# The first block's second mixer written as a pipeline in a kept order, one head a step, with scores from stacked fp32r parts

## The chip, the core and the metric

The kernel runs on one core of one Trainium2 chip. The metric is the device time of one execution in microseconds. PE is the matmul engine, DVE the vector engine, ACT the scalar engine, POOL the GpSimd engine and SP the engine that issues most DMAs.

## What is computed

The whole program is two blocks of two layers on 256 positions of width 1024. The change is in the mixer of the first block's second layer: an input projection, 16 heads with three attention branches each (compressed, selected, window), and an output projection. At 256 positions all four blocks of 64 are selected and the window covers everything, so the selected and the window branch are both causal attention, over keys of their own (`ks`, `kw`).

```python
def nsa_mixer(h, w_in, b_gate, q_g, k_g, cmp_pos, cmp_w1, cmp_w2, rel_table, w_out):
    q, kc, vc, ks, vs, kw, vw, gl = jnp.split(h @ w_in, splits, axis=-1)
    q = rms_norm(q.reshape(B, S, G, J, Dh), q_g)
    ks = rms_norm(ks, k_g[1])
    kw = rms_norm(kw, k_g[2])
    gates = jax.nn.sigmoid((gl + b_gate).astype(f32)).reshape(B, S, G, J, 3)
    Kc = rms_norm(compress(kc, cmp_pos[0], cmp_w1[0], cmp_w2[0]), k_g[0])
    Vc = compress(vc, cmp_pos[1], cmp_w1[1], cmp_w2[1])
    s_c = jnp.einsum('bsgjd,bngd->bgjsn', q, Kc) * scale + table[...]
    p_c = masked_softmax(s_c, ends[None, :] <= tpos[:, None])
    o_c = jnp.einsum('bgjsn,bngd->bsgjd', p_c, Vc)
    ...
    s = jnp.einsum('bqgjd,bqgnld->bgjqnl', qi, Kg) * scale + bias      # selected blocks
    o_s = jnp.einsum('bgjqnl,bgqnld->bqgjd', masked_softmax(s, m), Vg)
    ...
    s = jnp.einsum('bqgjd,bkgd->bgjqk', qi, kb) * scale + bias_w       # window
    o_w = jnp.einsum('bgjqk,bkgd->bqgjd', masked_softmax(s, mask), vb)
    ...
    o = gates[..., 0:1] * o_c + gates[..., 1:2] * o_s + gates[..., 2:3] * o_w
    return o.reshape(B, S, NSA_WIDTH) @ w_out
```

## The kernel before

`odd_mixer` computes this mixer. Weights come in **units** of 128x1024: `E.units` loads two units in one DMA, and `E.split` (L171) makes of each an fp32r high part `w_hi` (a copy on ACT, L175) and a low part `w_lo` (a subtraction on DVE or POOL, L166; `E.pattern` says which). A unit is 24 matmuls of 128x256 in fp32r: `mm3` (L201) issues three products for each of eight blocks.

The stage that the change touches begins when the keys, the values and the gates have been computed. Eight query units fill `q` (four in each call of `queries`); after each, `head_stat` adds the sum of squares with a small matmul, and after four the factors of the normalization are worked out by `rstd` and `rows` (L254 to L259, L369, L370), spread over the partitions by `spread2` (L386) and multiplied in. `attend(a)` then runs eight heads. It first computes the compressed branch of all eight (L1282 to L1305), and then for each head: two score matmuls in plain fp32 with a contraction of 64 (L1314, L1316), four DVE operations that add the bias and find the maximum (L1327), four exponentials on ACT with their sums (L1329), the scaling by gate and sum (L1331 to L1336), six transposes (L1339 to L1341) with two copies out (`pts`, L1344 on ACT and L1346 on DVE), and five matmuls with the values into `pv` (L1348 to L1351). After every second head `E.parts` reads `pv` into `yh` (ACT, L488) and `yl` (DVE, L489). Eight output units then accumulate into `acc` from `yh` and `yl`.

The order is the scheduler's: it may move instructions across heads and units. The pools limit it: the scores have two PSUM buffers (`at`), the transposes one (`tp`), `pv` one, the weights three of `w_hi` and three of `w_lo`.

## Time and profile before

| | us |
|---|---|
| median of 3 runs | 3491.49 (3486.87 to 3491.85) |
| the profiled execution | 3472.96 |
| its span, first to last instruction | 3471.2 |
| PE busy | 3306.5 (95%) |
| DVE busy | 2408.9 (69%) |
| ACT busy | 1895.5 (55%) |
| POOL busy | 944.4 (27%) |

The span holds all stages. The stage of this change lies at about 1114 to 1265 us, one twenty-third of it. PE counts as busy from the start of a matmul to its modelled end, so a stage with PE near 100% can still hold slow matmuls; what a matmul costs is better read from the distance between the starts of two neighbours.

### The profile page before, as it was taken

To read this page: it belongs to the slowest core of one execution; us is meant where nothing else is said; L and a number is where in the kernel's file an instruction comes from. 1 tells how busy PE (TensorE), PEld (TensorE's weight loads), DVE (VectorE), ACT (ScalarE), POOL (GpSimd) and SP (SyncE) were. 2 spreads that over 40 slices of the span, in tenths; PEclk is the share of its full clock that TensorE was granted. 3 is DMA by queue.
4 is the path that set the end of the run, shared out by engine and by line. 5 is a ranking of instruction groups with operands and counts; after the bars stand their busy time and mean duration, and the time that the engine had idled before them with its cause. 6 is when DMAs were issued, how large, how long until landed. Compare 5 with 4: busy or idle time off the path is not lost.

```text
span 3471.2 us, 64306 instructions
## 1 busy us (share of the span) xinstructions
PE 3306.5 (95%) x25971; PEld 3122.5 (90%) x25971; DVE 2408.9 (69%) x4479; ACT 1895.5 (55%) x3609; POOL 944.4 (27%) x470
## 2 busy tenths in 40 slices
PE   5889999999998999999999999999989999999899
PEld 4679999999997679999999999987869999878799
DVE  5777878888885567878867776576655454776644
ACT  3445677644445555677644445456654454565543
POOL 1034000044444135000044444442142232312422
PEclk8989999999999999999999999999999999999999
DMA  6535444477774124444345555543325555423354
GB/s 244 182 126 183 170 146 146 146 260 273 274 261 167 43 81 171 174 147 149 144 178 186 190 184 194 185 159 113 122 88 193 183 182 182 152 98 134 108 184 146
DMA packets 85979, 576.90 MB, mean 166 GB/s; under 512 B 9919, under 2 KB 11312, under 8 KB 20144
## 3 DMA queue, kind: packets, MB, share of 16 engines
q1 hardware_dynamic: 82448, 567.35, 45.7%
q8 instruction: 203, 3.33, 0.4%
q0 software_dynamic: 1648, 3.56, 0.4%
q10 hardware_dynamic: 1584, 1.88, 0.2%
q14 instruction: 96, 0.79, 0.1%
HBM read 571.80 MB, written 1.34 MB: 165 GB/s over the span
## 4 chain that ended last, share of the span: by engine, by line
PE 82%; DVE 9%; ACT 4%; issue 1%; DMA 1%; POOL 1%; ACTq 0%; DVEq 0%; POOLq 0%
PE acc L204 14%; PE acc L203 14%; PE acc L205 14%; PE mm L204 9%; PE mm L203 9%; PE mm L205 9%; PE g L1003 2%; ACT w_hi L175 2%; PE g L1005 2%; DVE w_lo L166 1%; DMA w_raw<-peer_v 1%; DVE m L1543 1%; DVE wl L489 1%; DVE xl L290 1%; DVE sql L489 1%
## 5 line engine op out<-in xcount | busy, mean ns | idle before, releaser
L175 ACT ACTIVATE w_hi<-w_raw 128x1024 fp32r<-128x1024 f32 x980 | 1037.6, 1059 | 968.9 <-PE acc L204 404.1
L166 POOL TENSOR_TENSOR w_lo<-w_raw,w_hi 128x1024 fp32r<-128x1024 f32 x357 | 865.0, 2424 | 2301.1 <-ACT w_hi L175 1507.7
L166 DVE TENSOR_TENSOR w_lo<-w_raw,w_hi 128x1024 fp32r<-128x1024 f32 x623 | 766.9, 1231 | 316.2 <-ACT w_hi L175 298.9
L203 PE MATMUL mm<-xh,w_hi 128*128 128x256 f32 (+1 forms) x2568 | 730.8, 285 | 15.2 <-ACT xh L336 7.1
L204 PE MATMUL mm<-xl,w_hi 128*128 128x256 f32 (+1 forms) x2568 | 731.8, 285 | 3.6 <-DVE xl L290 1.6
L205 PE MATMUL mm<-xh,w_lo 128*128 128x256 f32 (+1 forms) x2568 | 729.0, 284 | 2.2 <-DVE w_lo L166 2.2
L204 PE MATMUL acc<-wl,w_hi 128*128 128x256 f32 x2048 | 574.8, 281 | 8.1 <-DVE wl L489 8.0
L203 PE MATMUL acc<-wh,w_hi 128*128 128x256 f32 x2048 | 574.1, 280 | 3.3 <-ACT wh L488 3.3
L205 PE MATMUL acc<-wh,w_lo 128*128 128x256 f32 x2048 | 573.8, 280 | 0.0
L203 PEld LDWEIGHTS mm<-xh,w_hi 128*128 128x128 f32 (+1 forms) x2568 | 489.3, 191 | 23.3 <-issue 11.6
L204 PEld LDWEIGHTS mm<-xl,w_hi 128*128 128x128 f32 (+1 forms) x2568 | 489.0, 190 | 10.3 <-DVE xl L290 5.3
L205 PEld LDWEIGHTS mm<-xh,w_lo 128*128 128x128 f32 (+1 forms) x2568 | 489.3, 191 | 5.0 <-DVE w_lo L166 3.4
L203 PE MATMUL acc<-xh,w_hi 128*128 128x256 f32 (+1 forms) x1536 | 445.4, 290 | 11.6 <-DVE x L447 6.3
L204 PE MATMUL acc<-xl,w_hi 128*128 128x256 f32 (+1 forms) x1536 | 441.1, 287 | 15.5 <-DVE xl L558 15.0
L489 DVE TENSOR_TENSOR wl<-ring,wh 128x256 fp32r<-128x256 f32 x256 | 360.0, 1410 | 122.8 <-ACT wh L488 122.6
L205 PE MATMUL acc<-xh,w_lo 128*128 128x256 f32 (+1 forms) x1536 | 438.2, 285 | 0.1
L204 PEld LDWEIGHTS acc<-wl,w_hi 128*128 128x128 f32 x2048 | 385.9, 188 | 9.9 <-DVE wl L489 9.9
L203 PEld LDWEIGHTS acc<-wh,w_hi 128*128 128x128 f32 x2048 | 385.9, 188 | 3.7 <-ACT wh L488 3.7
L205 PEld LDWEIGHTS acc<-wh,w_lo 128*128 128x128 f32 x2048 | 385.9, 188 | 0.0
L204 PEld LDWEIGHTS acc<-xl,w_hi 128*128 128x128 f32 x1536 | 296.4, 193 | 19.0 <-DVE xl L558 16.9
L203 PEld LDWEIGHTS acc<-xh,w_hi 128*128 128x128 f32 x1536 | 298.1, 194 | 14.1 <-ACT xh L556 6.3
L205 PEld LDWEIGHTS acc<-xh,w_lo 128*128 128x128 f32 x1536 | 295.5, 192 | 1.3 <-DVE w_lo L166 0.4
(464 smaller groups left out, 5923.4 us busy)
## 6 DMA issues: line engine op xcount, KB each, us to landing
w_raw<-ffn SPq DMA_DIRECT2D x132, 1024.0 KB, 4.8
w_raw<-peer_u SPq DMA_DIRECT2D x128, 1024.0 KB, 4.8
w_raw<-peer_v SPq DMA_DIRECT2D x128, 1024.0 KB, 4.8
w_raw<-mix_in SPq DMA_DIRECT2D x48, 1024.0 KB, 4.8
ring<-ada SPq DMA_DIRECT2D x56, 512.0 KB, 5.8
ada<-ada SPq DMA_DIRECT2D x20, 1024.0 KB, 4.8
w_raw<-mix_out SPq DMA_DIRECT2D x16, 1024.0 KB, 4.8
w_raw<-even_in SPq DMA_DIRECT2D x12, 1024.0 KB, 6.8
```

The source lines that it names most:

```text
L166: ins = e.tensor_tensor(out, a, hi, op=OP.subtract)
L175: self.nc.scalar.activation(hi[:, :n], src, AF.Copy)
L203: mm(ps, wh, xh, start=start, stop=False, skip_group_check=True)
L204: mm(ps, wh, xl, start=False, stop=False, skip_group_check=True)
L205: mm(ps, wl, xh, start=False, stop=stop, skip_group_check=True)
L290: nc.vector.scalar_tensor_tensor(self.xl[:, c], self.x[:, c], a(c), self.xh[:, c].bitcast(F32), op0=OP.mult, op1=OP.subtract)
L489: return self.nc.vector.tensor_tensor(yl, src, yh.bitcast(F32), op=OP.subtract).ins
L1003: nc.tensor.matmul(ps[:, t], oi[:, :, t], o1[:, :, t], start=t == 0, stop=False, skip_group_check=True)
L1005: nc.tensor.matmul(ps[:, t], oi[:, :, t], o2[:, :, t], start=False, stop=t == TB - 1, skip_group_check=True)
L1543: nc.vector.scalar_tensor_tensor(m[:, sl], m[:, sl], col[:, 3 + k, h:h + 1], cbm[:, g, sl], op0=OP.mult, op1=OP.mult)
```

## The change

The stage becomes a pipeline whose order is kept as written on PE, DVE and ACT (`E.in_order`, which was there before and is used elsewhere). Three things are new.

**Scores from stacked parts.** `keys` splits the keys of a group into fp32r high and low parts, each on both halves of the partitions (`ksh`, `ksl`); `stack` puts the high part of a head's queries on one half of the partitions and the low part on the other (`qs`). `scores` then has four fp32r matmuls with a contraction of 128 (two of 256 columns, two of 512) in the place of two fp32 matmuls with a contraction of 64.

**One head a step.** Step `i` scales head `i-1`, multiplies head `i-2` with the values, turns head `i-1` (transposes), weighs head `i` (bias, maximum, exponentials), and computes the scores of head `i+1`. In steps 0 to 3 and from 8 on, half a unit of weights (12 matmuls) stands between the two turns: the last two query units, then the output units; the last three output units stand alone at the end. `scale`, `weigh`, `turn` and `values` are the old operations in functions of their own; `factors` and `scaled` are the normalization's two halves, `stats` its small matmuls.

**Where weights are split.** `Flow` splits a unit when one is finished (`flow.split`), with all subtractions on DVE. `units` at the end of an odd step is such a place.

```diff
+        qs = S.tile([128, 16, T], F32R, name="qs")
...
-            C = ctx3.enter_context(tc.tile_pool(name="cmp", bufs=1, reuse_waits="tile"))
+            C = ctxc.enter_context(tc.tile_pool(name="cmp", bufs=1, reuse_waits="tile"))
...
+        P = ctx.enter_context(tc.tile_pool(name="odp", bufs=1, reuse_waits="tile"))
+        ks = [P.tile([128, 4, 512], F32R, name=n) for n in ("ksh", "ksl")]
+        ctx.enter_context(E.in_order(*(e.engine for e in (nc.tensor, nc.vector, nc.scalar))))
+        flow = Flow(E, chain(units, E.units(io["odd_out"])), 2)
+        squares, heads, pcts, pvs = deque(), {}, {}, {}
+        def keys(g):
+            a, o = g // 2, g % 2 * 64
+            key, hi = kcat[o:o + 64, a], ks[0][o:o + 64, g]
+            for to in (o, 64 - o):
+                nc.scalar.activation(ks[0][to:to + 64, g], key, AF.Copy)
+            for to in (o, 64 - o):
+                nc.vector.tensor_tensor(ks[1][to:to + 64, g], key, hi.bitcast(F32), op=OP.subtract)
+        def keep(u, ps):
+            nc.scalar.activation(turned(q[:, u]), tiles(ps), AF.Copy)
+            sq = E.nrm.tile([128, T], F32, name="sq", bufs=4)
+            nc.scalar.activation(sq, q[:, u], AF.Square)
+            squares.append((u % 4, sq))
...
+        def stack(u):
+            for hf in range(2):
+                o = 64 * hf
+                nc.scalar.activation(qs[o:o + 64, 2 * u + hf], q[o:o + 64, u], AF.Copy)
+            for hf in range(2):
+                o = 64 * hf
+                nc.vector.tensor_tensor(qs[64 - o:128 - o, 2 * u + hf], q[o:o + 64, u],
+                                        qs[o:o + 64, 2 * u + hf].bitcast(F32), op=OP.subtract)
...
-                    mm_(s0[:, :256], q[o:o + 64, u, 0:128], kcat[o:o + 64, a, 0:256], start=True, stop=True)
-                    mm_(s1, q[o:o + 64, u, 128:256], kcat[o:o + 64, a], start=True, stop=True)
...
+        def scores(i):
+            a, j, hf, u, h = place(i)
+            qh = qs[:, 2 * u + hf]
+            s0, s1 = (at.tile([128, 512], F32, name="at") for _ in range(2))
+            for ps, ts, n in ((s0[:, :256], slice(0, 128), 256), (s1, slice(128, 256), 512)):
+                for k in range(2):
+                    mm_(ps, qh[:, ts], ks[k][:, 2 * a + hf, :n], start=k == 0, stop=k == 1)
...
+        def unit():
+            n, w = counter[0], next(flow)
+            counter[0] += 1
+            if n < 8:
...
+                    E.mm3(ps, w[0][:, c * 128:c * 128 + 128], ..., c == 0, c == NB - 1)
+                    if c == 3:
+                        yield
+                flow.split()
+                keep(n, ps)
+            else:
...
+                    E.mm3(acc[n // 2][:, n % 2], w[0][:, sl], w[1][:, sl], yh[:, k], yl[:, k], ...)
+                    if n == 3:
+                        yield
+                flow.split()
+            yield
...
-        queries(0)
-        attend(0)
-        queries(1)
...
-        attend(1)
-        E.pattern = "P"
-        units = E.units(io["odd_out"])
-        for k in range(8):
-            E.accum(acc, next(units), yh[:, k], yl[:, k], k == 0, k == 7)
+        for u in range(4):
+            for _ in unit():
+                pass
+            stats(stat, 1)
+            keys(u)
+        fill = unit()
+        next(fill)
+        stats(stat)
+        r = factors(stat, rows[0])
+        next(fill)
+        fill = unit()
+        next(fill)
+        for us in ((0, 1), (2, 3)):
+            scaled(0, r, us)
+        next(fill)
+        stack(0)
...
+        comp = compressed(0)
+        next(comp)
+        scores(0)
+        next(comp)
+        next(comp, None)
+        for i in range(18):
+            if i == 8:
+                ctx3.close()
+                acc = E.accs(...)
+            if 0 <= i - 1 < 16:
+                scale(i - 1)
+            if 0 <= i - 2 < 16:
+                values(i - 2)
+            if 0 <= i - 1 < 16:
+                turn(i - 1, 0)
+            done = i >= 3 and i % 2 == 1
+            if done:
+                u = (i - 2) // 2
+                nc.scalar.activation(yh[:, u], pvs[u], AF.Copy)
+            if i < 16:
+                weigh(i)
+            filled = i < 4 or i >= 8
+            if filled:
+                if i % 2 == 0 or i >= 16:
+                    fill = unit()
+                next(fill)
+            if 0 <= i - 1 < 16:
+                turn(i - 1, 1)
+            if done:
+                nc.vector.tensor_tensor(yl[:, u], pvs[u], yh[:, u].bitcast(F32), op=OP.subtract)
+            if i % 2 == 0 and i < 14:
+                stack(i // 2 + 1)
+            if i >= 16:
+                next(fill)
+            if i < 15:
+                scores(i + 1)
+            if i == 2:
+                stats(stat)
+            elif i == 4:
+                stats(stat)
+                r = factors(stat, rows[1])
+            elif i == 5:
+                for us in ((0, 1), (2, 3)):
+                    scaled(1, r, us)
+                comp = compressed(1)
+                next(comp)
...
+        while counter[0] < 16:
+            for _ in unit():
+                pass
```

The words below: `p_...` are a head's weights before and after scaling, `at` its scores, `pv` the output of two heads, `y_...` the parts `yh` and `yl`, `nm` and `sm` maxima and sums.

On DVE, around the reading of `pv` after every second head, before and then now:

```order
L1327 ISA p_13896,nm<-at,bias 128x2x128
L1327 ISA nm 128x1
L489 TENSOR_TENSOR y_12433<-pv,y_12433 128x256 [waits Activation_49]
L1331 RECIPROCAL sm<-sm 128x4 [waits Activation_49]
L1332 TENSOR_TENSOR sm<-sm,gates 128x4 [waits DVE_49]
L1336 TENSOR_SCALAR p_13895<-p_13895,sm 128x128 [waits DVE_49]
```

```order
L1375 ISA p_14080,nm<-at,bias 128x2x128
L1375 ISA nm 128x1
L166 TENSOR_TENSOR w_lo<-w_raw,w_hi 128x1024 [waits DMAHW5_49,Activation_49]
L1490 TENSOR_TENSOR y_12433<-pv,y_12433 128x256 [waits PE_49]
L1383 RECIPROCAL sm<-sm 128x4
L1384 TENSOR_TENSOR sm<-sm,gates 128x4 [waits DVE_49]
L1388 TENSOR_SCALAR p_14079<-p_14079,sm 128x128 [waits DVE_49]
```

A subtraction for weights, which waits for ACT, now stands ahead of the one that reads `pv` last.

On ACT, before and then now, around a copy `w_hi` in the second half of the heads (the exponentials of one head are four rows):

```order
L1329 ACTIVATE p_14016,sm<-p_14016,nm 128x2x128 [waits DVE_49]
L175 ACTIVATE w_hi<-w_raw 128x1024 [waits DMAHW6_49,PE_49,Pool_49]
L488 ACTIVATE y_12433<-pv 128x256 [waits PE_49]
L1344 ACTIVATE pts<-tp 128x3x128 [waits PE_49,Activation_49]
L1344 ACTIVATE pts<-tp 128x3x128 [waits DVE_49,PE_49,Activation_49]
```

```order
L1399 ACTIVATE pts<-tp 128x3x128 [waits PE_49,Activation_49]
L1479 ACTIVATE y_12433<-pv 128x256
L1377 ACTIVATE p_14079,sm<-p_14079,nm 128x128 [waits DVE_49]
L1377 ACTIVATE p_14080,sm<-p_14080,nm 128x2x128 [waits DVE_49]
L1377 ACTIVATE p_14079,sm<-p_14079,nm 128x128 [waits DVE_49]
L1377 ACTIVATE p_14080,sm<-p_14080,nm 128x2x128 [waits DVE_49]
L175 ACTIVATE w_hi<-w_raw 128x1024 [waits DMAHW5_49]
L1399 ACTIVATE pts<-tp 128x3x128 [waits PE_49,Activation_49] x2
```

The copy `w_hi` now stands behind the four exponentials of the step and ahead of the copies `pts` of the next turns.

On PE, in the second half of the heads, before (matmuls of a unit stand between the pieces of a head, some in the middle of three products) and then now:

```order
L1314 MATMUL at<-kcat,q 128x256 [waits DVE_49]
L1316 MATMUL at<-kcat,q 128x512 [waits DVE_49]
L1348 MATMUL pv<-pts,vr 64x256 [waits DVE_49,Activation_49]
L1349 MATMUL pv<-pts,vr 64x128
L1339 MATMUL tp<-cst,p_13814 128x128 [waits PE_49]
L1340 MATMUL tp<-cst,p_13815 128x128
L1341 MATMUL tp<-cst,p_13815 128x128
L205 MATMUL acc_13698<-y_12433,w_lo 128x256
```

```order
L1358 MATMUL at<-ksh,qs 128x256 [waits DVE_49]
L1358 MATMUL at<-ksl,qs 128x256
L1358 MATMUL at<-ksh,qs 128x512 [waits DVE_49]
L1358 MATMUL at<-ksl,qs 128x512
L1411 MATMUL pv<-pts,vr 64x256 [waits DVE_49]
L1412 MATMUL pv<-pts,vr 64x128
L1411 MATMUL pv<-pts,vr 64x256 [waits Activation_49]
L1412 MATMUL pv<-pts,vr 64x128
L1413 MATMUL pv<-pct_13756,vcr 64x256
L1393 MATMUL tp<-cst,p_13843 128x128 [waits DVE_49,PE_49]
```

The scores are four rows, the five matmuls of a head with the values stand in one piece, and the first of them waits for DVE; no matmul of a unit stands between the scores and that one.

## Rows read from the trace of the kernel before

**Rows 1.** Windows: us, busy and instructions of PE, PEld, DVE, ACT, POOL; clock, DMA.
```profile
1114.50:1143.80 29.30, 29.27 (x214) 25.11 (x214) 10.14 (x24) 14.23 (x28) 5.21 (x4) 1.00 0.28 99
1143.80:1197.20 53.40, 50.34 (x252) 29.27 (x251) 33.42 (x142) 27.72 (x88) 7.42 (x4) 1.00 0.07 26
1197.20:1257.20 60.00, 58.58 (x282) 37.10 (x281) 30.73 (x131) 26.78 (x83) 11.48 (x5) 0.89 0.11 36
1257.20:1265.40 8.20, 8.15 (x67) 7.95 (x66) 3.70 (x7) 4.37 (x7) 2.28 (x2) 1.00 0.36 128
```

**Rows 2.** Timeline of PE, most of one head: start, us, operation.
```profile
1167.65 0.65 PE L1348 MATMUL pv<-pts,vr 128*64 128x256 f32 x2
...
1168.45 0.64 PE L1351 MATMUL pv<-pct,vcr 32*64 32x256 f32 x2
1169.02 0.33 PE L1339 MATMUL tp<-cst,p 128*128 128x128 f32 x1
...
1169.49 0.70 PE L1314 MATMUL at<-kcat,q 64*128 64x256 f32 x2
1170.12 0.39 PE L204 MATMUL mm<-xl,w_hi 128*128 128x256 f32 x1
1170.44 1.12 PE L1316 MATMUL at<-kcat,q 64*128 64x512 f32 x2
1171.49 0.65 PE L1348 MATMUL pv<-pts,vr 128*64 128x256 f32 x2
```

**Rows 3.** Windows around two stretches of lower clock, columns as in group 1.
```profile
1200.40:1214.10 13.70, 13.70 (x44) 8.71 (x43) 8.18 (x37) 6.62 (x23) 2.36 (x1) 0.52 0.07 13
...
1279.00:1282.30 3.30, 0.85 (x8) 0.64 (x6) 3.15 (x4) 0.00 (x0) 2.37 (x1) 0.92 0.41 174
1282.30:1289.10 6.80, 5.79 (x27) 5.50 (x28) 6.80 (x15) 4.53 (x9) 2.84 (x1) 0.54 0.44 157
```

**Rows 4.** Timeline of PE: fp32r matmuls of 512 columns; next stage's first matmul.
```profile
1098.05 0.40 PE L233 MATMUL mm<-w_hi,xh 128*128 128x512 f32 x1
1098.29 0.39 PE L234 MATMUL mm<-w_lo,xh 128*128 128x512 f32 x1
...
1265.48 0.39 PE L203 MATMUL acc<-xh,w_hi 128*128 128x258 f32 x1
```

**Rows 5.** DVE: timeline of one head, then groups of the stage (busy us, mean ns).
```profile
1219.27 0.28 DVE L1327 CUSTOM_DVE_ANT_0 p<-at,bias 128x128 f32<-128x128 f32 x1
...
1221.57 0.18 DVE L1331 RECIPROCAL sm<-sm 128x4 f32<-128x4 f32 x1 [1.11 <-ACT p L1329]
...
1221.98 1.01 DVE L1336 TENSOR_SCALAR p<-p,sm 128x128 f32<-128x128 f32 x4
...
L166 DVE TENSOR_TENSOR w_lo<-w_raw,w_hi 128x1024 fp32r<-128x1024 f32 x4 | 4.9, 1226 | 5.6 <-ACT w_hi L175 5.6
...
L489 DVE TENSOR_TENSOR y<-pv,y 128x256 fp32r<-128x256 f32 x8 | 3.4, 425 | 10.1 <-ACT y L488 10.1
```

**Rows 6.** ACT: timeline of one head's exponentials, then groups of the stage.
```profile
1219.67 0.40 ACT L1329 ACTIVATE p<-p,nm 128x128 f32<-128x128 f32 x1 [3.42 <-DVE nm L1327]
...
1221.44 0.47 ACT L1344 ACTIVATE pts<-tp 128x384 f32<-128x384 f32 x1
...
L175 ACT ACTIVATE w_hi<-w_raw 128x1024 fp32r<-128x1024 f32 x15 | 15.8, 1056 | 13.0 <-PE mm L204 6.2 <-PE acc L204 5.5 <-issue 1.2
...
L254 ACT ACT_TABLE_LOAD x2 | 2.6, 1283 | 0.0
```

**Rows 7.** Timeline: half the compression, compressed scores on PE; the normalization's factors on DVE.
```profile
1117.96 4.32 PE L1237 MATMUL tp<-k,w 128*64 128x75 f32 x32
...
1144.42 1.30 PE L1282 MATMUL tp<-KcT,q 128*128 128x32 f32 x10
...
1137.49 0.41 DVE L256 TENSOR_SCALAR rs_v<-stat 8x256 f32<-8x256 f32 x1 [4.32 <-ACT rs_r L254]
...
1140.68 0.42 DVE L370 TENSOR_TENSOR rq<-rs_v,rq 8x256 fp32r<-8x256 f32 x1
```

166 lines of the change are left out of this document (98 added, 68 removed).

## Prediction

> **What bounds the kernel now.** I read the windows first, cut where the stage's work changes [rows 1]. The stage runs from 1114.5 us to the next stage's first matmul at 1265.5 [rows 4], 151.0 us. In all four windows PE is busy nearly throughout (29.27 of 29.30, 50.34 of 53.40, 58.58 of 60.00, 8.15 of 8.20), so only 4.5 us lie open; DVE and ACT are near half. PE bounds the stage, in an order that the scheduler has packed: wherever a head waits, matmuls of a unit run.
>
> Then PE's timeline, for what a head costs; the distance between starts is the price [rows 2]. The first score matmul takes 0.63 (1169.49 to 1170.12), the second 1.05 (1170.44 to 1171.49): 1.68 us a head. Three transposes take 0.47, or 0.30 ahead of an fp32r matmul, six 0.6. A head's values take 0.80 for one branch, as much for the other and 0.57 for the compressed one: 2.15. A unit's matmul takes 0.12 (67 in 8.15 us, the last of rows 1), twelve with the change of type at both ends 1.6.
>
> Last the clock. From 1200.4 to 1214.1 the granted clock is 0.52 of full speed, that is 1.2 of 2.4 GHz for nearly all of it [rows 3]: 13.7 us in which PE's work needs twice its time, so about 6.6 us of the 151 are lost. The windows ahead of it held PE's only real waits (50.34 of 53.40 busy). After a stretch with 0.85 us of matmuls in 3.30 it falls again, from 1282.3 to 1289.1. A stage that keeps PE waiting pays twice here.
>
> **The change part by part.**
>
> *Scores.* Four fp32r matmuls replace the two fp32 ones. At 512 columns one takes 0.24 (1098.05 to 1098.29) [rows 4], at 256 columns 0.12: 0.71, and with the change of type 0.85 us a head in the place of 1.68. Over 16 heads PE is relieved of 13 us.
>
> *Parts of keys and queries.* Eight copies and eight subtractions of 64x512 for the keys, sixteen of each of 64x256 for the queries. None of this exact shape is in the trace; by the 128x256 subtraction at 0.43 and the 128x1024 one at 1.23 [rows 5] the large cost about 0.6 and the small 0.35 each, 10 us on DVE and as much on ACT. Both engines are busy half of the stage [rows 1], so most of it could hide; what it costs lies in where it stands.
>
> *The kept order.* I walked the new order step by step, each instruction starting when its engine is free and its inputs are there. A head costs DVE 1.2 us for the weighing (1219.27 to about 1220.45) and 1.4 for the scaling, of which the half that lets the first turn begin is done after 0.95 [rows 5]; it costs ACT 1.76 for the exponentials (1219.67 to 1221.44), 0.4 for a copy after a turn, and every second head 0.3 for `yh` and 1.0 for a `w_hi` [rows 6]. These sums, with the parts and copies 4.0 us a head on DVE and 3.3 on ACT, are below PE's 5.2 (values 2.15, half a unit 1.6, two turns 0.6, scores 0.85). By throughput PE stays the bound. By order it does not:
>
> An odd step of the second half goes like this. Its values end on PE at 2.15 and its first turn at 2.45 (us from the step's start). ACT then copies the turn (2.9) and `yh` (3.2), runs the four exponentials (4.95), and only then the copy `w_hi` (5.95). DVE's subtraction for the same unit waits for that and ends at 7.2; behind it in DVE's queue stands the reading of `pv` (7.55). PE has by then finished its half unit, the second turn and the scores at 5.2, and its next instruction is the values of the next head, which write the one `pv`. It waits 2.4 us; behind it on PE wait both turns, half a unit and the scores. The even step that follows has no such chain, 5.2. An odd and an even step together take 12.8 in which PE has 10.4 of work.
>
> So the stage adds up, at full clock:
> - To the end of the compressed branch's turn, 37.1 us (1114.5 to 1151.6): 30.4 of PE's work (six query units 17.1; the second half of the compression 4.3 [rows 7], with its small products and `vcr` 6.2; five `stats`, the spreading, the compressed scores at 0.125 each [rows 7], head 0's scores, that turn) and 6.7 of waits. These are 2.1 for the second unit's squares, which stand on ACT behind the key parts and a `w_hi`; 1.4 for the factors, 2.5 of DVE work in six operations [rows 7] that stand behind the key subtractions; 2.2 for the compressed softmax, eight small DVE steps of 0.2 to 0.4, the larger ones taken like the 0.43 of [rows 5], that nothing covers now; the rest 1.0.
> - Steps 0 to 8, 56.2: 40.7 of work and 15.5 of waits. 3.6 of these fall at step 5, where the second factors, between two table loads of 1.28 [rows 6], stand ahead of the scaling; 2.4 at step 4 behind `pv`; 1.9 at step 1; 1.5 at step 5, where the spreading waits for DVE; 1.6 at step 7; the rest in eight smaller ones.
> - Three pairs of steps from step 9 to 14: 3 x 12.8 = 38.4.
> - From step 15 to the end 24.3: its own wait behind `pv`, three heads' values, and 4.5 units, the last three of which nothing delays.
>
> Sum 156.0 against 151.0: five more, although the old 151.0 hold 6.6 lost to the clock and the new score matmuls save 13. The waits come to 32 us where they were 4.5.
>
> *The clock in the new order.* Before, waits of 3 us in 53 preceded 13.7 us of half clock [rows 1, 3]. The new order waits more and in longer pieces: at the compressed softmax and step 1, at steps 4 to 7, and 2.4 us in each of four odd steps. I bound its cost from none to seven stretches like that of 6.8 us at 0.54, which loses 3.1 if all of it were matmuls on the path [rows 3]: 0 to 22. Waits take up part of such a loss, and not every wait brings one. I take 8, six stretches of 1.3, nearer to the lower end.
>
> The rule that speaks against this change is in the Trainium skill, TensorE: Matmul & The Clock Gate, section "HAM oscillation — how this bites in real kernels": bursts of matmuls with waits between them let the array fall back to its lower clock again and again, so that each burst starts slow. The row at 1282.3, slow behind a stretch almost without matmuls, agrees; the window 1143.8 to 1197.2, 3 us of waits at full clock, says that short ones are forgiven for a time. By the rule the sum would be at its upper end, the third rival.
>
> *Subtractions off POOL.* All weights of the stage are now subtracted on DVE, 1.23 each; twelve more by the two orders, in the sums above. POOL's 26 us fall away at no gain, since nothing waited for them on the path.
>
> *Behind the stage* the order is as before; the last output units and the residual's first steps stand alike. I cost it at nothing.
>
> So the profiled time of 3472.96 would become 3472.96 + 5 + 8 = 3486. That execution lay 18.5 below the median of the timed runs, 3491.49; what is added should be the same there: 3491.5 + 13 = 3504.
>
> **Rivals.**
>
> 1. *Dense after all, faster.* If the subtraction for weights were ready early enough (the copy `w_hi` needs only an old load and a free buffer) and DVE and ACT ran ahead, the four waits behind `pv` would vanish (9.6), and half of the others with them (11); with no clock lost that is 151.0 to 135.4, so 3476. For it: both engines have over 1 us of slack a step. Against it: the order is kept, and in it the copy stands behind the exponentials. It decides if the waits stay below 27 us at full clock, beside 124 of work.
>
> 2. *The waits as walked, but the clock holds:* + 5, 3496.5, which is no measurable change. For it: in the profile 50.34 of 53.40 busy held full clock for 53 us. Against it: the new waits are ten times as many.
>
> 3. *The clock falls at every pair:* four stretches of 6.8 us there, three before, each losing 3.1: + 5 + 22, 3518.
>
> 4. *The stacked scores save nothing:* + 13 + 13, 3517. Against it: the 512-column row at 0.24.
>
> **How the numbers follow.** Forecast (waits as walked, the clock falls in some of them; + 7 to + 19) 0.47; rival 1 0.12; rival 2 0.20; rival 3 0.18; rival 4 0.03. A change below 0.2%, 7 us, is about what a measurement of this kernel can't tell from none. Slower by more than that: forecast nearly all, rivals 3 and 4, together 0.66; same 0.23, rival 2 and the forecast's lower edge; faster 0.11, most of rival 1. The range that leaves out the faster half of rival 1 and the upper tail of rival 3 goes from 3487 to 3519.
>
> **What the new profile would show.** Right: score matmuls 0.24 apart or less; on PE the matmul on `pv` of an even head as the line that waits longest, released by DVE; odd and even steps together 12 to 14 us; a wait of 3 us or more at the second factors; several stretches of the clock near 0.5; a stage from the second compression to the residual of 160 us or more. Wrong: PE busy as densely as before in the second half, or the clock at 1.00 through all of the stage. What would make it wrong most easily is the clock, of which only the past stretches tell, and a subtraction of weights that starts earlier than I let it.

## The result, and the profile after

| | before | changed |
|---|---|---|
| median (us) | 3491.49 (3479.72 to 3496.30, 5 runs) | 3504.44 (3499.42 to 3513.68, 5 runs) |
| ratio | | 1.0054, 95% interval 1.0034 to 1.0074 |
| profiled execution | 3472.96 | 3499.42 |

The kernel became slower by half a per cent. The medians lie 13 us apart, the ratio says 18.9 us (11.9 to 25.8). The predicted time was 3504.0; that this agrees to half a microsecond is partly luck, as is told below.

The windows of the changed kernel, cut where the prediction cut its sum: the stage up to the end of the compressed branch's turn, steps 0 to 8, steps 9 to 14, the rest up to the last output matmul, and from there to the next stage's first projection; under them the six stretches of half clock in the stage (0.50 in the column of the clock, 1.2 of 2.4 GHz). Columns as in [rows 1].

```profile
1115.20:1153.40 38.20, 32.96 (x226) 28.28 (x225) 22.34 (x51) 20.50 (x38) 0.00 (x0) 0.92 0.25 83
1153.40:1215.98 62.58, 49.76 (x247) 34.87 (x246) 35.04 (x149) 33.24 (x108) 0.53 (x1) 0.80 0.05 18
1215.98:1256.10 40.12, 31.48 (x193) 23.21 (x194) 23.48 (x100) 20.59 (x69) 0.00 (x0) 0.96 0.07 27
1256.10:1281.90 25.80, 22.33 (x150) 18.41 (x150) 10.31 (x31) 10.43 (x22) 1.87 (x1) 0.93 0.24 82
1281.90:1305.60 23.70, 15.10 (x99) 14.09 (x99) 16.18 (x25) 11.59 (x23) 14.08 (x11) 0.86 0.30 96
...
1133.80:1137.20 3.40, 3.40 (x16) 3.23 (x16) 2.88 (x5) 3.30 (x7) 0.00 (x0) 0.50 0.65 207
1150.90:1157.70 6.80, 4.93 (x20) 4.24 (x20) 3.61 (x17) 3.17 (x12) 0.53 (x1) 0.50 0.22 94
1185.00:1198.70 13.70, 10.91 (x40) 8.45 (x40) 8.01 (x36) 4.28 (x12) 0.00 (x0) 0.50 0.00 1
1205.50:1212.30 6.80, 6.16 (x21) 3.83 (x20) 5.27 (x28) 3.48 (x12) 0.00 (x0) 0.50 0.01 2
1236.20:1239.60 3.40, 2.85 (x9) 1.74 (x10) 2.85 (x16) 0.00 (x0) 0.00 (x0) 0.50 0.60 210
1263.50:1266.90 3.40, 3.17 (x9) 1.93 (x10) 1.43 (x7) 0.00 (x0) 0.00 (x0) 0.50 0.71 241
```

Where before all windows but one showed PE busy nearly throughout [rows 1], PE is now open for 5.2, 12.8, 8.6 and 3.5 us in the four windows of the stage, 30.2 in all against 4.5. The six stretches of half clock add up to 37.5 us with PE busy in 31.4 of them, against one of 13.7 [rows 3].

What PE waited for in the stage and up to the next one, from the view of waits (total us, times, longest):

```profile
PE pv L1411 <- DVE y L1490: 14.9, 5, 3.4
PE tp L1393 <- DVE p L1388: 6.1, 3, 3.8
PE acc L203 <- DVE x L447: 4.4, 2, 2.6
PE mm L1342 <- DVE pc L1338: 2.8, 1, 2.8
PE mm L203 <- ACT xh L336: 2.4, 1, 2.4
PE stat L1290 <- ACT sq L1284: 2.3, 1, 2.3
```

And one odd step followed by its even one, from the timelines of PE, ACT and DVE (start, us, operation, idle time before it and who ended it):

```profile
1242.19 0.36 PE L1358 MATMUL at<-ksh,qs 128*128 128x256 f32 x1
...
1243.06 0.65 PE L1411 MATMUL pv<-pts,vr 128*64 128x256 f32 x2
...
1251.02 0.65 PE L1411 MATMUL pv<-pts,vr 128*64 128x256 f32 x2 [2.88 <-DVE y L1490]
...
1247.85 0.49 ACT L1377 ACTIVATE p<-p,nm 128x256 f32<-128x256 f32 x1
...
1248.34 1.04 ACT L175 ACTIVATE w_hi<-w_raw 128x1024 fp32r<-128x1024 f32 x1
...
1249.41 1.22 DVE L166 TENSOR_TENSOR w_lo<-w_raw,w_hi 128x1024 fp32r<-128x1024 f32 x1 [2.66 <-ACT w_hi L175]
1250.55 0.42 DVE L1490 TENSOR_TENSOR y<-pv,y 128x256 fp32r<-128x256 f32 x1
```

This is the chain of the prediction, link by link: the last exponential, the copy `w_hi`, the subtraction that DVE stood idle for, the reading of `pv`, and then PE's values of the even step, which start 7.96 us after those of the odd one (1243.06 to 1251.02). A head's scores take 0.87 (1242.19 to 1243.06) where they took 1.68 [rows 2].

**What comes behind the stage.** The last two windows' border is the last output matmul. From there to the next projection it took 17.5 us before (1265.4 to 1282.9, PE busy 13.8) and 23.7 now. DVE's timeline at that place, in the kernel before:

```profile
1263.24 2.05 DVE L447 SCALAR_TENSOR_TENSOR x<-acc,mods,x 128x256 f32<-128x256 f32 x5 [1.36 <-PE acc L205]
1265.46 1.21 DVE L290 SCALAR_TENSOR_TENSOR xl<-x,mcol,xh 128x256 fp32r<-128x256 f32 x2 [0.17 <-ACT xh L289]
```

and in the changed one:

```profile
1281.61 0.83 DVE L302 TENSOR_TENSOR xl<-mods,xh 128x16 fp32r<-128x16 f32 x1 [2.99 <-ACT xh L301]
1282.36 0.47 DVE L447 SCALAR_TENSOR_TENSOR x<-acc,mods,x 128x256 f32<-128x256 f32 x1
1283.41 0.48 DVE L290 SCALAR_TENSOR_TENSOR xl<-x,mcol,xh 128x256 fp32r<-128x256 f32 x1 [0.57 <-ACT xh L289]
1283.81 0.48 DVE L447 SCALAR_TENSOR_TENSOR x<-acc,mods,x 128x256 f32<-128x256 f32 x1
```

Before, DVE began the residual (L447) 2 us ahead of the end of the output matmuls and took five of its eight chunks in one go. Now it begins half a microsecond behind them (the last one starts at 1281.57 and takes 0.28), after a small subtraction that waited for ACT, and takes residual and parts in turns, waiting for ACT at each. The kept order is entered on the context of the whole mixer, so the residual and the first steps of the next norm stand in it too.

### The profile page after: what moved, and what is told of

Its sections match the earlier page's. It is cut to its first block, busy times and chain, and to the rows that moved or that the text cites. A ratio compares the mean times of both kernels' runs of the same rounds, so it can differ in the third digit from the quotient of the medians.

```text
span 3497.6 us, 64370 instructions
## 1 busy us (share of the span) xinstructions
PE 3303.6 (94%) x25971; PEld 3133.0 (90%) x25971; DVE 2418.5 (69%) x4506; ACT 1909.4 (55%) x3641; POOL 915.9 (26%) x459
## 4 chain that ended last, share of the span: by engine, by line
PE 58%; DVE 6%; ACT 4%; issue 1%; POOL 0%; ACTq 0%; DVEq 0%; POOLq 0%
PE acc L203 9%; PE acc L204 9%; PE acc L205 9%; PE mm L204 7%; PE mm L203 7%; PE mm L205 7%; ACT w_hi L175 1%; PE g L1003 1%; PE g L1005 1%; DVE w_lo L166 1%; DVE m L1692 1%; DVE sql L489 1%; DVE xl L290 1%; PE mm L234 1%; PE mm L235 1%
## 5 line engine op out<-in xcount | busy, mean ns | idle before, releaser
L166 POOL TENSOR_TENSOR w_lo<-w_raw,w_hi 128x1024 fp32r<-128x1024 f32 x346 | 836.1, 2417 | 2306.1 <-ACT w_hi L175 1517.4
L166 DVE TENSOR_TENSOR w_lo<-w_raw,w_hi 128x1024 fp32r<-128x1024 f32 x634 | 778.7, 1228 | 333.3 <-ACT w_hi L175 315.0
```

The lines of the kernel that those rows point to most:

```text
L166: ins = e.tensor_tensor(out, a, hi, op=OP.subtract)
```

## The experiments

All times of a stage below are cut alike: from the end of the last 512-column matmul ahead of the stage to the end of the last output matmul. This stage begins 4.3 us earlier than the one of the prediction, whose 151.0 and 166.7 us are 155.3 and 171.0 here. Waits are the window less PE's busy time, the clock is the mean granted one as a share of full speed, the residual goes from the stage's end to the next projection. Ratios are to the kernel before, run on the same chip beside each.

| kernel | ratio, 95% interval | stage | PE waits | mean clock | residual |
|---|---|---|---|---|---|
| before, two profiles | | 155.3, 159.1 | 4.6, 4.4 | 0.96, 0.92 | 17.5, 17.5 |
| changed, two profiles | 1.0054 (1.0034 to 1.0074), 1.0048 (1.0032 to 1.0065) | 171.0, 171.3 | 30.2, 30.2 | 0.89, 0.89 | 23.7, 23.6 |
| order ends with the stage (e1) | 1.0057 (1.0037 to 1.0078) | 170.8 | 30.3 | 0.90 | 17.4 |
| `yl` first (e2) | 1.0034 (1.0021 to 1.0047) | 160.9 | 21.6 | 0.92 | 23.6 |
| both, and `w_hi` early (e7) | 1.0004 (0.9992 to 1.0015) | 160.2 | 16.4 | 0.87 | 17.4 |
| e7, second turns copied on DVE (e11) | 1.0000 (0.9987 to 1.0012) | 158.7 | 17.9 | 0.89 | 17.4 |
| changed, scheduler's order (e3) | 0.9972 (0.9961 to 0.9983) | 143.0 | 8.1 | 0.95 | 17.4 |
| before, stacked scores (e4) | 0.9956 (0.9938 to 0.9973) | 143.2 | 8.8 | 0.98 | 17.5 |
| changed, fp32 scores (e6) | 1.0083 (1.0066 to 1.0099) | 184.9 | 16.1 | 0.81 | 22.5 |
| changed, extra matmuls in the waits (e9) | 1.0032 (1.0019 to 1.0046) | 164.2 | 15.1 | 0.97 | 22.5 |
| fp32 scores, extra matmuls (e10) | 1.0040 (1.0025 to 1.0055) | 164.9 | 7.7 | 0.97 | 23.7 |
| changed, `w_lo` on POOL (e8) | 1.0021 (1.0009 to 1.0032) | 164.2 | 22.8 | 0.90 | 22.6 |

### The kept order or the scores: two parts taken one at a time

e3 is the changed kernel without its kept order:

```diff
-        ctx.enter_context(E.in_order(*(e.engine for e in (nc.tensor, nc.vector, nc.scalar))))
```

> The changed kernel's code without the kept order: the same instructions, stacked scores and parts included, put in order by the scheduler. Theory (the order costs what the scores save): PE is filled wherever a head waits; the stage takes 151 less the 13 of the scores, and less what the clock no longer loses, 130 to 140 us where the changed kernel takes 170, and the ratio to the kernel before is 0.995 to 0.997. Rival (the parts of keys and queries, 10 us each on DVE and ACT, or the splitting of weights on DVE alone are what costs): waits for DVE and ACT remain, the stage stays above 150 us and the ratio at 1.000 or above.

e4 is the kernel before with the stacked scores (`keys`, `stack`, `qs` and `ks` as in the change):

```diff
-                    mm_(s0[:, :256], q[o:o + 64, u, 0:128], kcat[o:o + 64, a, 0:256], start=True, stop=True)
...
-                    mm_(s1, q[o:o + 64, u, 128:256], kcat[o:o + 64, a], start=True, stop=True)
...
+                    for ps, ts, n in ((s0[:, :256], slice(0, 128), 256), (s1, slice(128, 256), 512)):
+                        for k in range(2):
+                            mm_(ps, qh[:, ts], ks[k][:, 2 * a + hf, :n], start=k == 0, stop=k == 1)
```

> The kernel before with one part of the change alone: the scores from stacked fp32r parts, with the copies and subtractions for the parts of keys and queries; order, weights' splitting and head by head structure are those of before. Theory: each head's scores fall from 1.68 to 0.85 us on PE, which bounds this stage; the copies and subtractions (10 us each on DVE and ACT, both about half busy) hide; the stage falls from 151 to 138 us, the ratio to 0.996 to 0.997. Rival: PE then waits for DVE and ACT, the clock falls more often, and the stage stays at 148 to 152, the ratio at 0.999 to 1.001.

The stage of e3, then that of e4 (windows, columns as above):

```profile
1118.80:1261.80 143.00, 134.93 (x844) 103.55 (x843) 91.60 (x332) 88.54 (x240) 2.47 (x2) 0.95 0.17 60
```

```profile
1119.60:1262.80 143.20, 134.38 (x843) 101.29 (x842) 90.67 (x329) 87.16 (x232) 26.64 (x13) 0.98 0.17 60
```

Both rivals fall. DVE and ACT carry 11 to 12 us more each than before and hide it: PE waits for 8 to 9 us where it waited for 4.5. The stage is 12 to 16 us shorter than in the two profiles of the kernel before (13 was expected), and both are faster as a whole. Part of that is the clock: the 13 us of relief lose about 4 to new waits, and e4 had 7 us at half clock in its stage where the two profiles of before had 14 and 24. e3's ratio lies just above the 0.995 to 0.997 that were expected, with 14 us at half clock in the stage, e4's just below its 0.996 to 0.997. So the stacked scores are a gain, and the kept order alone costs 28 us of stage against the same instructions in the scheduler's order, 22 of them waits. **e4 beats both kernels**: its median was 3469.72 beside 3487.33.

### The chain ahead of pv

e2 moves one statement, the subtraction that reads `pv`, from behind the half unit to ahead of it, so that on DVE it stands ahead of `w_lo`:

```diff
             if i < 16:
                 weigh(i)
+            if done:
+                nc.vector.tensor_tensor(yl[:, u], pvs[u], yh[:, u].bitcast(F32), op=OP.subtract)
             filled = i < 4 or i >= 8
...
-            if done:
-                nc.vector.tensor_tensor(yl[:, u], pvs[u], yh[:, u].bitcast(F32), op=OP.subtract)
```

> In every second step the subtraction that reads pv stands ahead of the weights' subtraction on DVE and not behind it; nothing else is changed. Theory (the values of the next head wait for pv behind w_hi, w_lo, yl): the wait of 2.9 us ahead of the values of an even head goes; next in line is the scaling, which now stands behind w_lo, so that the first turn waits about 1 us; an odd and an even step together fall from 13.4 to 14.3 us to about 12, five times, and the time by 8 to 10 us: 1.0025 times the kernel before. Rival (the wait only changes its place, since the copy w_hi is what is late and everything stands behind it): a pair stays above 13 us, the turn waits over 2 us, the ratio stays at 1.005. In the clock, the theory wants fewer stretches near 0.5 between 1220 and 1270 us than the two of 3.4 us there.

PE's timeline of e2, the first values of an even head, then a wait in the middle of them, and the same of the next pair:

```profile
1238.83 0.65 PE L1411 MATMUL pv<-pts,vr 128*64 128x256 f32 x2
1240.57 0.65 PE L1411 MATMUL pv<-pts,vr 128*64 128x256 f32 x2 [0.87 <-ACT pts L1399]
...
1250.16 0.65 PE L1411 MATMUL pv<-pts,vr 128*64 128x256 f32 x2
```

A pair takes 11.3 us (1238.83 to 1250.16) where the changed kernel's take 12.9 to 14.3; the wait of 2.9 is gone, the stage is 10 us shorter, no stretch of half clock is left in its second half, and the ratio fell by 0.0014 to 0.0020, a little less than expected (the intervals still overlap, so it is the trace that decides). The theory stands; what is late next is not the first turn, as expected, but the copy of the second one, which stands on ACT behind `w_hi`.

e7 moves the copy `w_hi` ahead of the exponentials as well (`copied` issues it and hands back the subtraction for later), and ends the kept order with the last output unit:

```diff
+            filled = i < 4 or i >= 8
+            todo = copied() if filled and i % 2 == 1 and i < 16 else []
             if i < 16:
                 weigh(i)
-            filled = i < 4 or i >= 8
+            if done:
+                nc.vector.tensor_tensor(yl[:, u], pvs[u], yh[:, u].bitcast(F32), op=OP.subtract)
+            for t in todo:
+                E.sub(*t)
...
         while counter[0] < 16:
             for _ in unit():
                 pass
+        kept.close()
```

> Three places in the order changed: the subtraction that reads pv ahead of the weights' one, the copy w_hi ahead of the exponentials of its step, and the kept order ending with the last output unit. Theory (waits at known places make up the loss): with w_hi ahead of the exponentials neither the reading of pv nor the copy after the next turn (0.9 us of wait in the run with yl first) is late, PE bounds the pairs at 10.4 to 10.9 us where that run has 11.3 and the changed kernel 13.4 to 14.3; the stage falls from 171 us to 157 to 160, the residual from 24.0 to 17.8, together 17 to 20 us below the changed kernel: 0.999 to 1.001 times the kernel before. Rival (with w_hi first the exponentials come 1 us later and the scaling behind them, so that the turn waits instead): the pairs stay at 11.3 or above, the ratio at 1.0015 to 1.003.

The ratio came out as the theory said (1.0004), the pairs did not: 11.04 us, with the same wait of 0.86. The reason can be seen in the order. The second turn's copy stands on ACT behind both the exponentials and `w_hi`, so their order doesn't matter to it. What e7 gains over e2 is nearly all in the residual: its stage has 5 us less of waits, but 41 us at half clock where e2 had 27. e11 takes that copy off ACT:

```diff
-            if br == 0 or i % 2 == 0:
+            if br == 0:
                 nc.scalar.activation(turned(pts), tiles(pt), AF.Copy)
             else:
                 nc.vector.tensor_copy(turned(pts), tiles(pt))
```

> As the run with both early and the order ending (yl and w_hi early, the kept order ending with the last output unit), and besides the copy after every second turn on DVE, where every other one was on ACT. In that run a pair of steps stayed at 11.3 us with a wait of 0.87 ahead of the values' second branch, since ACT's copy of the second turn stands behind both w_hi and the exponentials, whichever of them is first. Theory: with that copy on DVE, which ends its queue of the step at about 6.0 where PE needs it at 6.0, the 0.87 goes, a pair takes 10.4 to 10.6, four of them 3 us less, and the waits of the stage fall from 16.4 to 12 to 13 us; ratio 0.999 to 1.000. Rival (DVE becomes late with it, and the scaling behind): pairs at 11 or above.

PE's timeline of e11, the first values of two neighbouring odd steps, and between them a wait of the even one:

```profile
1230.83 0.65 PE L1412 MATMUL pv<-pts,vr 128*64 128x256 f32 x2
...
1237.15 0.65 PE L1412 MATMUL pv<-pts,vr 128*64 128x256 f32 x2 [0.47 <-DVE pts L1402]
...
1241.46 0.65 PE L1412 MATMUL pv<-pts,vr 128*64 128x256 f32 x2
```

10.63 us, close to what the theory said. PE's own work all but bounds the pairs now: of the wait of 0.87 there are 0.47 left, for the copy on DVE. The waits of the whole stage did not fall to 12 to 13 but are 17.9: at the second factors PE again waits 3.8, as in the changed kernel, where in e7 half clock had covered the place. Four repairs to the order have brought the kernel from 1.005 back to 1.000, and not to the 0.997 that the scheduler reaches with the same instructions (e3); what remains are the waits at the second unit's squares (2.3), the compressed softmax (2.8), the second factors (3.8) and step 7 (1.8), and 34 us at half clock in the stage.

### The clock

e9 puts matmuls that nobody reads ahead of the longest waits, 144 in all:

```diff
+        def busy(i, n):
+            for k in range(n):
+                mm_(heads[i][0][:, 256:], E.xh[:, 0, :128], E.xh[:, 1], start=True, stop=True, skip_group_check=True)
...
```

> The changed kernel with extra matmuls whose result nobody reads (256 columns, fp32r, 0.12 us each) on PE ahead of its longest waits: 18 at the compressed softmax, 8 at step 1, 20 at steps 3, 9, 11 and 13 ahead of the values, 26 and 12 at steps 5 and 7 ahead of the first turn. They fit into the waits (1.3 to 3.8 us each) if the clock is at full speed. Nothing else is changed; DVE and ACT have the same order. By the trace PE waits 30.1 us in the changed kernel's stage of 171.0; its work at full clock is the 131.5 that the stage of the kernel before has (155.2 less 4.4 of waits, 6.8 lost to the clock and 12 to 13 for the scores), so about 9.4 are lost to the clock. Theory (the waits let the clock fall, and this is paid beside them): with PE kept busy the stretches of half clock, 37.9 us in the stage, shrink to under 12, and the stage falls from 171 to 162 to 165, although PE has more to do; the time is 6 to 9 us below the changed kernel's: 1.002 to 1.003 times the kernel before. Rival (the stretches have another cause, or the extra matmuls end up on the path): the stage stays at 170 or grows, the ratio is 1.005 or above.

e10 does the same, with 100 matmuls, to the kept order with the old scores, which e6 runs without them. In both the copies and subtractions for the parts are left out as well:

```diff
-            for ps, ts, n in ((s0[:, :256], slice(0, 128), 256), (s1, slice(128, 256), 512)):
-                for k in range(2):
-                    mm_(ps, qh[:, ts], ks[k][:, 2 * a + hf, :n], start=k == 0, stop=k == 1)
+            mm_(s0[:, :256], q[o:o + 64, u, 0:128], kcat[o:o + 64, a, 0:256], start=True, stop=True)
+            mm_(s1, q[o:o + 64, u, 128:256], kcat[o:o + 64, a], start=True, stop=True)
...
```

> The kept order with the scores of before: two fp32 matmuls a head from q and kcat, without the copies and subtractions for the parts; all else as in the changed kernel. Theory (in the kept order part of the saving is lost, since the scores of every second step end ahead of a wait for pv that lasts 2.9 us whether they take 0.85 or 1.68): only the even steps and the first head lengthen, 8 to 9 times 0.83, 7 us, and the copies and subtractions that go give back 2 to 4 of that ahead of step 0 and at steps 1 and 7; so 2 to 6 us above the changed kernel of the same call. Rival (the saving arrives in full also here): 11 to 13 us above it. Second rival (the parts cost as much as they save): the same time or below.

> The kept order with the old fp32 scores and no parts, and the same extra matmuls ahead of the same waits, fewer of them (14, 6, 13 and 20 and 8) since the waits are shorter there. Without them this kernel's stage took 184.7 us with 16.0 of waits, against 171.0 and 30.1 with stacked scores: the waits shrank by 14 us, as much as the score matmuls grew, so at full clock both should take about the same, and the 13.7 between them would be the clock alone. Theory (in this order the stacked scores only turn work into waits): the stage falls to 161 to 167, within 3 us of the run with stacked scores and extra matmuls. Rival (the scores' time is on the path): it stays 8 us or more above that run.

The stages of e9, e6 and e10 (windows, columns as above):

```profile
1118.50:1282.70 164.20, 149.08 (x987) 120.65 (x986) 92.41 (x330) 87.75 (x240) 2.45 (x2) 0.97 0.15 52
```

```profile
1115.10:1300.00 184.90, 168.83 (x843) 118.87 (x842) 80.16 (x306) 76.46 (x216) 2.43 (x2) 0.81 0.13 46
```

```profile
1118.60:1283.50 164.90, 157.24 (x943) 117.01 (x942) 80.06 (x306) 76.35 (x216) 2.38 (x2) 0.97 0.15 52
```

In e9, 144 more matmuls in PE's count (987 against 843), some 17 us of work at 0.12 each, make the stage 7 us shorter, as the theory said: the mean clock rises from 0.89 to 0.97, with 10 us left at half clock in the stage. The three pairs from step 9 to 14 take 12.9 each now, where the changed kernel's took 12.9, 14.3 and 12.9: that 1.4 was the clock, the rest the wait. The whole time went the same way, from 1.0048 and 1.0054 to 1.0032, but these intervals overlap. So it is shown that in the changed kernel the half clock comes with the waits: with matmuls in them 27 of its 37.5 us are gone. How much half clock a given wait brings is not shown, as the next run tells.

e6 is a miss. I expected 2 to 6 us above the changed kernel, since the scores would only fill waits; it was 13.2 (3518.09 beside 3504.94), the rival's number. But the rival's reason is wrong too. The waits did shrink by 14.1 us (30.2 to 16.1), about as much as the score matmuls grew (16 times 0.83). What made the stage longer is the clock, 0.81, that is about 70 us at half of full speed. e10 settles it: with the clock kept up, fp32 scores (164.9) and stacked ones (164.2) take the same stage, and the whole times agree (3500.80 and 3499.47). In this order, at full clock, the stacked scores with their parts save nothing, since the waits grow as the work shrinks; as the kernels stand they save 13 us, by way of the clock. The fourth rival of the prediction, that they save nothing, holds only with the clock kept up, and by a mechanism that it didn't name.

### The end of the kept order, and subtractions on POOL

e1 only ends the order with the last output unit:

```diff
-        ctx.enter_context(E.in_order(*(e.engine for e in (nc.tensor, nc.vector, nc.scalar))))
+        kept = ctx.enter_context(ExitStack())
+        kept.enter_context(E.in_order(*(e.engine for e in (nc.tensor, nc.vector, nc.scalar))))
...
+        kept.close()
         E.pattern = "VVP"
         E.ada_add(48 + 16, 8)
```

> The kept order ends with the last output unit, so that the residual and the next stage's first instructions are the scheduler's again; nothing else is changed. Theory (the kept order also held these, and DVE and ACT took them one by one): from the first matmul of the next stage's norm back to the last output matmul PE waits 2.6 us in the changed kernel and not at all before, and from the last output matmul to the next stage's first projection it takes 24.0 us (1281.57 to 1305.57) where it took 17.8 (1265.07 to 1282.91). This should fall back to about 18, and the time by 6 us, or by up to 9 if the two stretches of half clock behind it (1307.9 to 1331.8) go as well: about 1.003 times the kernel before. Rival (the residual is late because the output units end late, or the clock fell there by chance): it stays at 24 and the ratio at 1.0054. The pairs of steps stay at 13 to 14 us in either case.

DVE's timeline of e1 at that place, and the window from the last output matmul to the next projection:

```profile
1285.80 2.05 DVE L447 SCALAR_TENSOR_TENSOR x<-acc,mods,x 128x256 f32<-128x256 f32 x5 [1.40 <-PE acc L205]
```

```profile
1288.00:1305.40 17.40, 13.74 (x98) 12.42 (x98) 16.92 (x19) 10.25 (x22) 13.45 (x11) 1.00 0.38 129
```

The residual again begins ahead of the last output matmul, and the window falls by 6.3 us to what it was. The whole time doesn't show it: 1.0057 (1.0037 to 1.0078), where 1.003 was expected, just outside the interval. In its profile other stretches hide the 6.3: what lies ahead of the stage, with the same matmuls in both, took 1117.2 us against 1110.9, and the program's rest from about 1472 us on took 2031.7 against 2025.3. e2, whose order ends where the changed kernel's does, has 1118.5 and 2031.2, so neither comes from where the order ends. The trace shows the effect here; the times of e1 do not confirm it. The step from e2 to e7, 1.0034 to 1.0004 with 0.7 us less in the stage, agrees with it. The stretches of half clock behind the residual remained, against the hope of 9.

e8 gives the weights' subtractions of the stage to POOL:

```diff
-                flow.split()
+                flow.split(pattern="P")
...
```

> The subtractions for weights of this stage on POOL (2.4 us each, outside the kept order) in the place of DVE (1.2 us each, within it); order else as in the changed kernel. Theory (pv's reading stands behind w_lo on DVE): with w_lo gone from DVE's queue the wait of 2.9 us goes just as it does with yl ahead of it, the scaling isn't delayed either, the copy after the turn behind w_hi keeps 0.9: pairs of 11.3, a stage of 158 to 161, 9 to 12 us below the changed kernel, 1.002 to 1.003 times the kernel before. Rival (moving the subtractions off POOL was free or a gain, and POOL at twice the time each makes PE wait for weights): waits of PE for w_lo appear, and the time is that of the changed kernel or above.

The pairs fall to 11.04 to 11.09, a little below the 11.3 that were expected, which confirms the chain ahead of `pv` from another side, and the ratio is inside what was expected. The stage is 3 us longer than expected: a new wait of 4.3 stands ahead of the first factors' spreading. DVE's timeline there, POOL's, and DVE's of the changed kernel at the same place:

```profile
1151.89 0.41 DVE L258 TENSOR_TENSOR rs_v<-rs_v,rs_r 8x256 f32<-8x256 f32 x1
1152.34 2.48 DVE L259 SCALAR_TENSOR_TENSOR rs_v<-rs_v,rs_r 8x256 f32<-8x256 f32 x1
1154.86 2.31 DVE L369 CAST rq<-rs_v 8x256 fp32r<-8x256 f32 x1
1157.20 0.42 DVE L370 TENSOR_TENSOR rq<-rs_v,rq 8x256 fp32r<-8x256 f32 x1
```

```profile
1151.99 5.03 POOL L166 TENSOR_TENSOR w_lo<-w_raw,w_hi 128x1024 fp32r<-128x1024 f32 x2 [3.39 <-ACT w_hi L175]
```

```profile
1143.11 0.41 DVE L259 SCALAR_TENSOR_TENSOR rs_v<-rs_v,rs_r 8x256 f32<-8x256 f32 x1
1143.55 0.28 DVE L369 CAST rq<-rs_v 8x256 fp32r<-8x256 f32 x1
```

The operations of 0.41 and 0.28 take 2.48 and 2.31 while POOL makes its two subtractions, and the next, begun behind POOL's end (1157.02), takes 0.42 again.

### Both kernels once more

> The changed kernel itself once more, beside the next three on the same chip, so that they have a ratio to stand against, and a second profile of it. Every theory expects 1.004 to 1.007 times the kernel before. What the second profile tells: whether the stretches of half clock fall in the same places. The theory that each follows a wait of the kept order expects them again near the compressed softmax, step 1, steps 5 to 8 and two of the four later pairs, 35 to 45 us in all in the stage; if they were chance, they lie elsewhere or come to less than 25.

> The kernel before once more, for a second profile of it. Over the eleven runs so far the stretch from the stage's start to a matmul some 335 us later is longer than in the one profile of before by 7 us more on the mean than the timed runs say (changed kernel: 27 us in the trace, 17 to 19 by the ratio). One guess: that profile was a lucky one there, and usually the kernel before also loses 5 us to a stretch of 13.7 us of half clock behind the stage, as eight of the eleven others did: then the new profile shows that stretch and 338 to 343 us where the old one has 334.6. If it was not luck, 333 to 336 again, and the 7 us are given back elsewhere. The stage itself should be 155 us in either case, with one stretch of 13.7 us of half clock in it.

The second profile of the changed kernel and that of the kernel before, stage, residual and the 166 us behind it:

```profile
1113.90:1285.20 171.30, 141.12 (x843) 108.96 (x842) 92.37 (x330) 87.75 (x240) 2.44 (x2) 0.89 0.14 50
1285.20:1308.80 23.60, 15.06 (x98) 14.05 (x98) 16.09 (x25) 11.50 (x23) 14.04 (x11) 0.86 0.29 97
1308.80:1475.50 166.70, 164.64 (x1318) 160.80 (x1318) 129.67 (x521) 85.36 (x138) 53.85 (x22) 0.95 0.47 164
```

```profile
1115.40:1274.50 159.10, 154.71 (x843) 105.57 (x842) 79.22 (x305) 76.02 (x208) 26.41 (x13) 0.92 0.15 54
1274.50:1292.00 17.50, 13.78 (x99) 12.45 (x99) 16.98 (x19) 10.34 (x23) 13.50 (x11) 1.00 0.41 131
1292.00:1458.50 166.50, 164.43 (x1318) 160.81 (x1318) 129.91 (x521) 84.48 (x138) 54.01 (x22) 0.95 0.47 164
```

The changed kernel repeats itself: the same waits in the stage to 0.02 us, and the same six stretches of half clock, all of it some 3 us later. The kernel before doesn't: its stage took 159.1 with two stretches of half clock (10.2 and 13.7 us) where the first profile had one, against the 155 that I expected, and behind the residual it lost 5 us that the first profile (1282.9 to 1444.5, 161.6 us) had not. So the profile that the prediction rests on had lost 9 us less to the clock there. Against this second profile the changed kernel's stage is 12 longer, the residual 6, the rest nothing: 18, which is what the ratios say (16.8 and 18.9).

## Why the prediction was right, and where it was not

| term (us) | predicted | measured |
|---|---|---|
| to the end of the compressed turn | 37.1, waits 6.7 | 38.2, waits 5.2 |
| steps 0 to 8 | 56.2, waits 15.5 | 62.6, waits 12.8 |
| steps 9 to 14 | 38.4, waits 2.4 each pair | 40.1, waits 2.9 each pair |
| step 15 to the end | 24.3 | 25.8 |
| lost to the clock | 8, six stretches | in the rows above: 9 to 16 by estimate, six stretches |
| stage | 164 | 166.7 |
| residual, to the next projection | nothing | + 6.2 |
| against the kernel before, all | + 13 | + 13 by medians, + 17 to 19 by ratios |

**Scores.** Predicted 0.85 a head, measured 0.87. One fp32 matmul of 512 columns cost 1.05, an fp32r one 0.24, a ratio of 4.4. The Trainium skill, FP8 and Floating Point Precision, section "TensorE Precision Notes", says that true fp32 makes four passes through the array. These rows agree. That 13 us of relief are a gain by themselves e4 showed (12 to 16 us less of stage, a part of it by the clock).

**Parts of keys and queries.** Estimated 0.6 and 0.35 on DVE, measured 0.69 and 0.42 (ACT 0.63 and 0.41): 12 us where I had 10. Hidden in the scheduler's order, as e3 and e4 show.

**The walk through the order.** This step carried the forecast and held: the wait behind `pv` in every second step (2.4 predicted, 2.9 measured, and 2.8 at step 4), the second factors (3.6, measured 3.8), the second unit's squares (2.1, 2.3), the compressed softmax (2.2, 2.8), step 7 (1.6, 1.8). Wrong were the first factors (1.4, measured 0.2) and step 1 (1.9, measured 0.5 at half clock, and 1.3 more a step later). In sum 30.2 against 32. e2, e7, e11 and e8 show the chain link by link.

**The clock.** Six stretches were predicted and six came; that the count agrees is in part luck, since the first (1133.8) follows the wait for the second unit's squares, where I had named none. They are longer than I took: PE was busy in 31.4 us of them, and half of that, 15.7, is an upper estimate of what matmuls took too long; the stage of before gave 9.4 (the expectation of e9). My 8 was too small by either. The stage is only 2.7 longer than forecast all the same. In part slow matmuls stood where PE would have waited: at step 1 the changed kernel waits 0.5 us in a stretch of half clock, and e9, at full clock there, 2.2. The rest depends on PE's work at full clock, of which I had summed 124: with 15.7 lost it was 120.8, with 9.4 it was 127.1, and no run decides between them. e9 shows the part that can be had back, 7 us. That every pair brings a fall was not borne out: two of the four later pairs show one. The Trainium skill, TensorE: Matmul & The Clock Gate, section "HAM oscillation — how this bites in real kernels", gives waits between bursts of matmuls, there for DMA, as the cause of slow starts. e9 agrees with it; e6 and e7, with about half the waits of the changed kernel and more half clock, show that the sum of the waits doesn't tell how much comes.

**Behind the stage: the step that failed.** "... the order is as before; the last output units and the residual's first steps stand alike. I cost it at nothing." It is not as before. The kept order reaches into the residual, which costs 6.2 us in both profiles of the changed kernel and goes away when the order ends earlier (e1, e7). The rows of DVE's order at the residual show it without any run: eight times `x` and `xl` in turns, where the scheduler had put five `x` in front. I compared the order in the stage and not behind it, and put the term at nothing.

**From the profile to the median: a second step that failed.** I carried the 18.5 us by which the profiled execution lay below the median over to the changed kernel. Its profile lay only 5.0 below its median. In the one profile of before, the stage and what follows had lost 9 us less to the clock than in the second (e12). So from the trace of before to that of after it is 26 us, where I had 13. The other 13 are the residual (6.2), the clock behind it (5.1), and 2.7 more in the stage than I summed, less 0.6 elsewhere. Against the second profile of before 18 are left, and the forecast of + 13 fell 4 to 6 us below what the ratios say; the agreement with the median to half a microsecond is luck, since a loss left out and a profile that happened to be fast lay behind it.

**The rivals.** Dense after all: no, 30 us of waits. The clock holds: no. A fall at every pair: half of them. That the scores save nothing: not by themselves (e4) and not in the kept order as it stands (e6), but in the kept order with the clock kept up (e9 and e10).

**Off POOL.** I wrote that nothing is gained by relieving POOL. e8 says more: putting the subtractions on DVE, within the order, cost 7 us of the stage (171.0 against 164.2).

## What to carry to other kernels

An order kept by hand is a queue on each engine: whatever reads the only copy of a buffer has to stand ahead of work that waits for a third engine, and one moved statement was worth 10 us here. Try the parts of a change one at a time, because a saving in matmuls inside an order that waits turns into waits: the same stacked scores gave 0.44% in the scheduler's order (e4) and nothing in the kept one once its clock was kept up (e9, e10). See where the scope of an order ends, and compare the order of instructions beyond the stage as well as in it.

## What the runs showed of the hardware that I had not expected

- More matmuls can be faster: 144 of no use in the waits raised the mean clock of the stage from 0.89 to 0.97 and shortened it from 171.0 to 164.2 us.
- Fewer waits don't always keep the clock up: fp32 scores in the kept order (e6) had half the waits of the stacked ones (16 against 30 us) and more half clock (mean 0.81 against 0.89), and so had e7 (16 us, 0.87). Why is open. The stretch of half clock behind the residual, 13.7 us in most profiles and absent in the first of before, in e4 and in e11, is not explained by the order either, since e3 has it.
- Two DVE operations of 0.41 and 0.28 us took 2.48 and 2.31 beside two subtractions on POOL (e8). The Trainium skill, SBUF — State Buffer, section "SBUF: two separate sides", describes a pair of ports shared by DVE and GpSimd, which one instruction holds to its end while the other is blocked. These rows agree with it: both operations ended within 0.3 us behind a subtraction (POOL's ended at 1154.54 and 1157.02).
- The kernel before, timed against itself, gave 0.9982 with an interval of 0.9966 to 0.9998. Differences of 0.2% aren't to be read from one such comparison.
